# Ranking the first stage's experts on the chip, and putting the second stream's combination behind the first's norm

## The chip, the cores and the metric

The kernel runs on one core of a Trainium2 chip, as one program. Its engines work side by side and wait for one another through semaphores: PE multiplies matrices, DVE and ACT work on rows of data, POOL issues the indirect transfers (gather and scatter of rows by an index table), and SP issues nearly all loads. The metric is device time in microseconds (us), the median of several runs. Each timing of the kernel before lies within about 0.5 us of the median, and 0.2% of it (3.0 us) is taken here as what a measurement can tell from no change.

## The reference

Two layers over 256 latent tokens and 256 context tokens of width 1024, in float32. Each layer is a mixer (conv, pooling, two kinds of attention) and then a mixture of experts, whose router sends each token to 2 of 16 experts. Only the latent stream is returned, so the second layer's mixture works on 256 tokens, and the first's on 512.

```python
for i in range(DEPTH):
    last = i == DEPTH - 1
    ...
    h2 = modulate(rms_norm(x, norm2[i]), sh2[:, None], sc2[:, None])
    tok = h2.reshape(b * n_lat, d)
    if not last:
        tok = jnp.concatenate([tok, h2c.reshape(b * n_ctx, d)], axis=0)
    y2 = moe_ffn(tok, w_router, b_router, w_gate[i], w_up[i], w_down[i])
    x = x + g2[:, None] * y2[:b * n_lat].reshape(b, n_lat, d)
...
# moe_ffn, for one block of tokens of expert e:
a = xblk @ w_gate[e]
u = xblk @ w_up[e]
y = (jax.nn.silu(a) * u) @ w_down[e]
```

An expert's three matrices are 1024x1024 in float32, 4 MB each: 12 MB an expert, 192 MB a layer. Which tokens an expert gets is data; the order in which the experts are worked off is free.

## The kernel before, in words

**The weights.** The class `Ring` (L983) streams the expert weights through 11 units of 2 MB each in the on-chip memory, so it holds a little under two experts. An expert is 12 loads of 1 MB: 4 pairs of gate and up, then 4 of down. All loads go through SP in program order, and `big_load` (its transfers are at L176) lets at most four be in flight: a load is issued when the one four before it has landed, and when the work that read the unit's old content is done. `ring.to(6 * e + 17)` behind expert e lets the stream run on to expert e + 2. SP and PE therefore run as a stream with a buffer between them, and the experts come in the order 0 to 15.

**The work of an expert in the first layer** (`moe0`, L1025). Tokens are handled in tiles of 32. For a tile, POOL gathers the rows of `h2d` (L1043), DVE transposes them (L1051), PE multiplies with gate and up (`gate_up`, L1014), ACT and DVE make silu(a) * u (L1020 to L1022), PE multiplies with down (L1066), ACT copies the result (L1054) and POOL scatters it to `yd` (L1047). Two tiles are always done. A third is done under a branch `v > 64` (L1128), a fourth under `v > 96` (L1133), and rest loops under `v > 128` (L1136). A light expert, with 64 tokens or fewer, takes the other arm of the first branch. Every engine takes these branches by itself, from counts that it has read into registers. [...]

**The router** (`router`, L792). For the last tile of tokens (`choose`, n = 3) DVE picks the experts, PE counts, and DVE turns the counts into the index tables `ig` (rows to gather) and `isx` (rows to scatter to). Then every engine reads 17 counts (L790) and branches on the largest one (L965), before expert 0 begins. DVE's work here and SP's work everywhere stand in the written order; on the other engines, and on DVE elsewhere, a scheduler orders the instructions.

**Behind the first layer's experts.** SP loads the second layer's constants (L260 to L276), parts of its input weights (`w_in`) and of the modulation weights (`w_mod`), then the four tiles of `yd` (L1164) once the last scatter has landed. `combine` (L1169) scales and adds a tile's two expert results, multiplies by a gate (L1173) and adds it to the stream (L1174). `attn_layer(1)` then takes the stream's norm: ACT squares and sums (L364), DVE makes the reciprocal root (`rsqrt`, L152 to L158), ACT scales (L369), PE transposes (L375) and DVE scales the columns (L383). It does so for stream 0 (tiles 0 and 1, latent) and then stream 1 (tiles 2 and 3, context).

**The end.** The second layer's experts (`moe1`, L1180) are another stream of 192 MB through the same ring.

Of the kernel before, what the change touches and what calls it, by code (L numbers as in the profile page):

```python
# [23 lines left out]
NE = 16  # L24
# [17 lines left out]
C_W = 1400  # L42
# [7 lines left out]
def const_layer(layer):  # L50
# [23 lines left out]
    c[:, C_II:C_II + 16] = (64 if layer else 32) * np.arange(16)[None, :]  # L74
    for i in range(4):
        for k in range(2):
            c[:, C_AV + 2 * i + k] = 128 * i + p + 1 if layer else 2 * (128 * i + p) + k + 1
# [22 lines left out]
def dit_moe_kernel(ctx: ExitStack, tc, x, c, cctx_tok, c_ctx, w_mod, b_mod, norm1, norm2, w_in, conv_w, w_pool,  # L100
# [50 lines left out]
    def rsqrt(y, v, hv, t):  # L151
# [3 lines left out]
        for _ in range(3):  # L155
            V.tensor_tensor(t, y, y, op=ALU.mult)
            V.tensor_tensor(t, t, hv, op=ALU.mult)
            V.scalar_tensor_tensor(y, t, 1.5, y, op0=ALU.subtract, op1=ALU.mult)  # L158
# [150 lines left out]
    def attn_layer(L, K, win_a, mid, prefetch, combine):  # L309
# [50 lines left out]
        scaled = None  # L360
        for s in order:
            for i in (2 * s, 2 * s + 1):
                scr = combine(i)
# [3 lines left out]
            rsqrt(stats(8 + k, 2), stats(4 + k, 2), stats(12 + k, 2), stats(16 + k, 2))  # L367
# [424 lines left out]
    def router(L, K, ts, H2):  # L792
# [6 lines left out]
        o = [2424 if L else C_W]  # L799
# [33 lines left out]
        else:  # L833
# [3 lines left out]
            tu = ru(3, 64)  # L837
        def select(e, pair, k):
# [32 lines left out]
        def choose(n, lg, shift):  # L871
# [26 lines left out]
            else:  # L898
                V.tensor_copy(cnt_i[:, 0:16], pp[:, 16:32])
                V.tensor_reduce(cnt_i[:, 16:17], cnt_i[:, 0:16], axis=AX.X, op=ALU.max)  # L900
            pv = pp[:, 0:16]
# [37 lines left out]
        def finish(full):  # L939
# [8 lines left out]
            V.tensor_scalar(ti, pb, -1.0, 0.0, op0=ALU.add, op1=ALU.max)  # L948
            V.tensor_scalar(ti, ti, -2, None, op0=ALU.bitwise_and)
            V.tensor_scalar(ig, ti, 2.0, CS[:, C_PG:C_PG + 1], op0=ALU.mult, op1=ALU.add)  # L950
# [9 lines left out]
            rows(pb, 0, I0, tu[:, 0], tu[:, 1])  # L960
# [3 lines left out]
            counts = read_counts(cnt_i, 512)  # L964
            with tc.If(counts[NE] > 32 * I0):  # L965
# [12 lines left out]
                rows(ps[:, 0:n], I0, I, m1[:, 0:n], m1[:, n:2 * n])  # L978
            return dict(counts=counts, ig=ig, isx=isx, gwt=gwt, pg=pg, at={i: n for n, i in enumerate(ts)})
# [3 lines left out]
    class Ring:  # L983
        def __init__(self, L):
# [3 lines left out]
            self.n = 0  # L988

        def to(self, n):  # L990
# [34 lines left out]
    def moe0(r, ring, tail, tables, late):  # L1025
        counts, ig, isx, gwt, pg, at = (r[n] for n in ("counts", "ig", "isx", "gwt", "pg", "at"))
# [75 lines left out]
        def fetch(e):  # L1102
            for i in range(3):
                gather(h2d, gi(i, e), i)
# [15 lines left out]
        for e in range(NE):  # L1120
            with tc.manual_schedule():
                v = counts[e]
# [46 lines left out]
        def combine(i):  # L1169
# [206 lines left out]
```

## Time and profile before

| | |
|---|---|
| median of the runs | 1521.66 us (1521.1 to 1522.02) |
| profiled execution, own time | 1518.51 us |
| its span, first to last instruction | 1516.9 us |
| PE busy | 1272.8 us, 84% |
| DVE, ACT, POOL busy | 32%, 16%, 11% |
| moved by the transfer engines | 513.45 MB, mean 338 GB/s |
| mean granted TensorE clock | 0.934 of full speed |

Busy shares are means over stages with different limits. What matters is, in each stage, whether the weights' stream runs at its full rate (then its GB/s stands at about 420 and PE waits for loads), or whether PE is behind it and the stream waits for units.

### The profile page before, as it was taken

To read this page: it belongs to the slowest core of one execution; us is meant where nothing else is said; L and a number is where in the kernel's file an instruction comes from. 1 tells how busy PE (TensorE), PEld (TensorE's weight loads), DVE (VectorE), ACT (ScalarE), POOL (GpSimd) and SP (SyncE) were. 2 spreads that over 40 slices of the span, in tenths; PEclk is the share of its full clock that TensorE was granted. 3 is DMA by queue.
4 is the path that set the end of the run, shared out by engine and by line. 5 is a ranking of instruction groups with operands and counts; after the bars stand their busy time and mean duration, and the time that the engine had idled before them with its cause. 6 is when DMAs were issued, how large, how long until landed. Compare 5 with 4: busy or idle time off the path is not lost. (4 is left out here: it accounts for less than half of the span.)

```text
span 1516.9 us, 24606 instructions
## 1 busy us (share of the span) xinstructions
PE 1272.8 (84%) x10006; PEld 595.2 (39%) x10006; DVE 492.7 (32%) x1360; ACT 236.0 (16%) x536; POOL 171.1 (11%) x271
## 2 busy tenths in 40 slices
PE   4998999969888877599999579998889798876778
PEld 1754555533333332244355247744223232221223
DVE  3465366671111111111111377857212221211211
ACT  4342134110000000000000255531000000000000
POOL 0411200002202111121212230300000000000000
PEclk9999979989999999899999779999999998999899
DMA  9677883466999999999988865376999999999995
GB/s 372 219 288 267 280 319 128 164 250 228 419 420 419 419 416 417 418 419 416 417 359 358 286 254 170 136 301 227 368 419 420 372 419 420 419 421 420 417 420 236
DMA packets 92828, 513.45 MB, mean 338 GB/s; under 512 B 16208, under 2 KB 19664, under 8 KB 36816
## 3 DMA queue, kind: packets, MB, share of 16 engines
q1 hardware_dynamic: 84320, 490.47, 80.8%
q0 software_dynamic: 6016, 16.98, 3.0%
q10 hardware_dynamic: 2288, 3.37, 0.6%
q8 instruction: 117, 1.92, 0.5%
q14 instruction: 87, 0.71, 0.1%
HBM read 502.46 MB, written 8.32 MB: 337 GB/s over the span
## 5 line engine op out<-in xcount | busy, mean ns | idle before, releaser
L1014 PE MATMUL psg<-u,W 128*32 128x512 f32 x4032 | 470.8, 611 | 71.8 <-DMA u<-in_w_up_dram 62.4
L1014 PEld LDWEIGHTS psg<-u,W 128*32 128x32 f32 x4032 | 151.0, 112 | 362.2 <-issue 311.3
L1021 DVE TENSOR_TENSOR W<-W,psg 128x256 f32<-128x256 f32 x63 | 26.5, 421 | 561.1 <-ACT W L1020 478.0
L1066 PE MATMUL pd<-u,W 128*32 128x256 f32 x2496 | 160.9, 399 | 41.8 <-issue 23.2
L1066 PEld LDWEIGHTS pd<-u,W 128*32 128x32 f32 x2496 | 93.1, 114 | 110.9 <-issue 54.5
L1216 PE MATMUL pd<-u,x 128*64 128x512 f32 x544 | 128.1, 626 | 2.5 <-DMA u<-in_w_gate_dram 1.9
L1020 ACT ACTIVATE W<-psg 128x256 f32<-128x256 f32 x63 | 24.2, 384 | 516.4 <-PE psg L1014 515.2
L754 PE MATMUL ps<-u,u 128*128 128x512 f32 x192 | 86.8, 598 | 0.0
L848 PE MATMUL pg<-W,x 128*32 128x256 f32 x544 | 46.0, 486 | 45.4 <-DVE x L840 39.1
L1047 POOL DMA_INDIRECT yd<-W x39 | 38.9, 998 | 385.4 <-ACT W L1054 345.6
L211 PE MATMUL psm<-u,W 128*32 128x512 f32 x320 | 48.5, 684 | 34.9 <-DMA u<-in_w_mod_dram 22.0
L1216 PEld LDWEIGHTS pd<-u,x 128*64 128x64 f32 x544 | 40.2, 145 | 86.0 <-issue 84.4
L1043 POOL DMA_INDIRECT W<-h2d,W x54 | 52.1, 965 | 118.7 <-DVE u L932 92.8
L326 DVE TENSOR_TENSOR x<-u,x 128x512 fp32r<-128x512 f32 (+2 forms) x64 | 42.1, 660 | 43.7 <-ACT x L325 39.3
L848 PEld LDWEIGHTS pg<-W,x 128*32 128x32 f32 x544 | 22.6, 130 | 73.0 <-issue 44.0
L325 ACT CAST x<-u 128x512 fp32r<-128x512 f32 (+2 forms) x64 | 35.4, 561 | 99.8 <-PE ps L400 48.6
L1051 DVE STREAM_TRANSPOSE W<-W 128x256 f32<-128x256 f32 x49 | 28.5, 627 | 68.5 <-PE pd L1066 45.9
L754 PEld LDWEIGHTS ps<-u,u 128*128 128x128 f32 x192 | 34.7, 190 | 37.2 <-issue 36.8
L1218 DVE SCALAR_TENSOR_TENSOR W<-pd,W,x 128x512 f32<-128x512 f32 x17 | 12.8, 751 | 111.5 <-PE pd L1216 111.5
L401 PE MATMUL ps<-u,x 128*128 128x512 f32 (+1 forms) x128 | 44.9, 351 | 1.5 <-DVE x L326 1.3
L399 PE MATMUL ps<-u,x 128*128 128x512 f32 (+1 forms) x128 | 45.1, 352 | 0.0
L400 PE MATMUL ps<-u,x 128*128 128x512 f32 (+1 forms) x128 | 44.4, 347 | 0.0
(276 smaller groups left out, 1347.3 us busy)
## 6 DMA issues: line engine op xcount, KB each, us to landing
u<-in_w_gate_dram SPq DMA_DIRECT2D x128, 1024.0 KB
u<-in_w_up_dram SPq DMA_DIRECT2D x128, 1024.0 KB
u<-in_w_down_dram SPq DMA_DIRECT2D x128, 1024.0 KB
u<-in_w_mod_dram SPq DMA_DIRECT2D x40, 1024.0 KB
u<-in_w_in_dram SPq DMA_DIRECT2D x12, 1024.0 KB
x<-in_w_mod_dram SPq DMA_DIRECT2D x8, 1024.0 KB
u<-in_w_out_dram SPq DMA_DIRECT2D x4, 2048.0 KB
u<-m_dram POOLq DMA_DIRECT2D x9, 512.0 KB, 8.8
```

Of the source, the lines that this page charges most:

```text
L211: PE.matmul(ps[32 * g:32 * g + 32, :], sc[:, j, :], t[:, 512 * g:512 * g + 512], start=(j == 0), stop=(j == 7), tile_position=(0, 32 * g))
L326: eng.tensor_tensor(l, src, h.bitcast(F32), op=ALU.subtract)
L399: PE.matmul(ps, xh, yh, start=first, stop=False)
L400: PE.matmul(ps, xh, yl, start=False, stop=False)
L401: PE.matmul(ps, xl, yh, start=False, stop=end)
L754: PE.matmul(ps, CT[:, k, 128 * i:128 * i + 128], wout[hh][:, k, :], start=(k == 0), stop=(k == 7))
L848: PE.matmul(pg[32 * g:32 * g + 32, 256 * i:256 * i + 256], OHG[k][:, c_, 32 * i:32 * i + 32].bitcast(F32), H2[c_][:, 256 * g:256 * g + 256 ...
L1014: PE.matmul(pss[k][32 * g:32 * g + 32, :], xTs[k][:, j, :], w[:, :, 256 * g:256 * g + 256], start=(j == 0), stop=(j == 7), tile_position=( ...
L1043: G.indirect_dma_start(out=XG[b], out_offset=None, in_=src, in_offset=bass.IndirectOffsetOnAxis(ap=ic, axis=0))
L1047: return G.indirect_dma_start(out=dst, out_offset=bass.IndirectOffsetOnAxis(ap=ic, axis=0), in_=src, in_offset=None)
L1066: PE.matmul(pd[32 * g:32 * g + 32, 0:256], hT[:, j, :], w[:, 256 * g:256 * g + 256], start=(j == 0), stop=(j == 7), tile_position=(0, 32 * g))
L1216: PE.matmul(pd[64 * h:64 * h + 64, :], HT[k][:, j, :], w[:, 512 * h:512 * h + 512], start=(j == 0), stop=(j == 7), tile_position=(0, 64 * h))
```

## The change

Experts 0 and 1 stay in front, since their weights are loaded before the router has run. The other 14 are ranked on the chip by their number of tokens, and take the places 2 to 15 in the order: most, fewest, second most, second fewest, and so on. DVE makes a permutation matrix `P`, and with it permutes the counts and the columns of both index tables; the experts' numbers in their new order go to SP, which reads them into registers and addresses the weights by them. Expert 0's first gathers use a small table `ig0` made ahead of the ranking. The 17 counts are no longer read before expert 0: the largest one is read there (`most`), and the 16 counts, now in the new order, behind expert 0's first down product; expert 0's branch has no hint any more. In the second layer's norm, the first DVE operation of `combine` for tiles 2 and 3 is ordered behind the last operation of stream 0's `rsqrt`; that sets an order on DVE and adds no wait.

```diff
+    c[:, C_RK:C_RK + 16] = np.where(q < 2, q, np.where(q % 2 == 0, 1 + q // 2, 16 - q // 2))[None, :]
...
-                scr = combine(i)
+                scr = combine(i, normed) if last else combine(i)
...
-            rsqrt(stats(8 + k, 2), stats(4 + k, 2), stats(12 + k, 2), stats(16 + k, 2))
+            normed = rsqrt(stats(8 + k, 2), stats(4 + k, 2), stats(12 + k, 2), stats(16 + k, 2))
...
+                V.tensor_copy(cf, pp[:, 16:32])
+                V.tensor_reduce(cmax, cf, axis=AX.X, op=ALU.max)
+                V.scalar_tensor_tensor(key, cf, 16.0, e16, op0=ALU.mult, op1=ALU.add)
+                for e in range(2):
+                    V.tensor_scalar(key[:, e:e + 1], key[:, e:e + 1], (2 - e) * 65536.0, None, op0=ALU.add)
...
+            rows_in(ig0, pb[:, 0::16], ti[:, 0:4])
+            V.tensor_copy(cnt_i[:, 16:17], cmax)
...
+            V.tensor_tensor(cmp, pair(key, 1), pair(key, 0), op=ALU.is_gt)
+            V.tensor_reduce(rank, cmp, axis=AX.X, op=ALU.add)
+            V.tensor_tensor(P, pair(CS[:, C_RK:C_RK + 16], 0), pair(rank, 1), op=ALU.is_equal)
+            for src, dst, a, b in ((e16, eid, -1.0, 16.0), (cf, cnt_i[:, 0:16], 1.0, 0.0)):
+                V.tensor_tensor(cmp, P, pair(src, 1), op=ALU.mult)
+                V.tensor_reduce(tot, cmp, axis=AX.X, op=ALU.add)
+                V.tensor_scalar(dst, tot, a, b, op0=ALU.mult, op1=ALU.add)
+            order = nc.values_load_multi_w_load_instructions(
+                eid[0:1, 0:16], engines=(ET.SP,), min_val=0, max_val=15,
+                skip_runtime_bounds_check_because="a permutation of the experts")[1]
+            pbs = tu[:, 1]
+            for i in range(I0):
+                V.tensor_tensor(cmp, P, pair(pb[:, 16 * i:16 * i + 16], 1), op=ALU.mult)
+                V.tensor_reduce(pbs[:, 16 * i:16 * i + 16], cmp, axis=AX.X, op=ALU.add)
+            rows_in(ig, pbs, ti)
...
-            counts = read_counts(cnt_i, 512)
-            with tc.If(counts[NE] > 32 * I0):
+            most = nc.values_load_multi_w_load_instructions(cnt_i[0:1, NE:NE + 1], min_val=0, max_val=512)[1][0]
+            with tc.If(most > 32 * I0):
...
-                src = dict(g=w_gate, u=w_up, d=w_down)[nm][self.L, e].rearrange("(p j) n -> p j n", j=8)[:, 2 * h:2 * h + 2, :]
+                at = ds(self.order[e], 1) if self.order and e > 1 else slice(e, e + 1)
+                src = dict(g=w_gate, u=w_up, d=w_down)[nm][self.L, at].rearrange("o (p j) n -> p (o j) n", j=8)[:, 2 * h:2 * h + 2, :]
...
-                gather(h2d, gi(i, e), i)
+                gather(h2d, gi(i, e) if e else ig0[:, i:i + 1], i)
...
-                tc.mark_branch_hint_location(f"more{e}", v > 64, engines=[ET.PE])
+                if e:
+                    tc.mark_branch_hint_location(f"more{e}", counts[e] > 64, engines=[ET.PE])
                 gu(e, [0, 1], [0, 1], [None, None])
                 dn(e, 0, "t")
-                with tc.If(v > 64, label=f"more{e}") as cmp:
+                if not e:
+                    counts.extend(r["read"]())
+                v = counts[e]
+                with tc.If(v > 64, **({"label": f"more{e}"} if e else {})) as cmp:
...
-            V.scalar_tensor_tensor(t, Yt[i][:, 1], gwt[:, 1, at[i]:at[i] + 1], t, op0=ALU.mult, op1=ALU.add)
+            j = V.scalar_tensor_tensor(t, Yt[i][:, 1], gwt[:, 1, at[i]:at[i] + 1], t, op0=ALU.mult, op1=ALU.add)
+            if before is not None:
+                behind(j, before)
```

Three places where the order of instructions moves. First, DVE between the router and expert 0. Before, it reads the counts and branches, and only then makes the three transposes of expert 0's first tiles (the rows between are the branch's body, for a count over 128):

```order
L963 COPY st<-u_63 128x1
L790 TENSOR_LOAD st
L965 COMPARE_AND_BRANCH
...
L965 UNCONDITIONAL_BRANCH x2
L1051 STREAM_TRANSPOSE W<-W 128x256 x3
```

In the change, two of the transposes (now L1101) stand in the middle of the ranking (L978 to L984 rank and permute, L990 and L991 permute the index table), well ahead of the read (L1006) and the branch:

```order
L978 TENSOR_TENSOR W<-u_63 128x256
L979 TENSOR_REDUCE W<-W 128x16
L980 TENSOR_TENSOR W<-u_63,W 128x256
L982 TENSOR_TENSOR W<-W,u_63 128x256
L983 TENSOR_REDUCE W<-W 128x16
L984 TENSOR_SCALAR W<-W 128x16
L982 TENSOR_TENSOR W<-W,u_63 128x256
L1101 STREAM_TRANSPOSE W<-W 128x256
L983 TENSOR_REDUCE W<-W 128x16
L984 TENSOR_SCALAR st<-W 128x16
L990 TENSOR_TENSOR W<-W,pb 128x256
L1101 STREAM_TRANSPOSE W<-W 128x256
```

So the transposes no longer wait for the counts, but the second one has more of DVE's work ahead of it.

Second, PE at expert 0. Before, the read and the branch come ahead of its first product with gate and up (L1014):

```order
L927 MATMUL pb<-W,u_63 128x64 x2
L790 TENSOR_LOAD st
L1125 REGISTER_ALU
L1371 BRANCH_PREFETCH_HINT
L965 COMPARE_AND_BRANCH
```

In the change (gate and up L1062) the first products stand ahead of the read of the largest count, and the others behind its branch:

```order
L944 MATMUL pb<-W,u_63 128x64 x2
L1062 MATMUL psg<-u_71,W 32x512 x8
L1062 MATMUL psg<-u_6_1290,W 32x512 x4
L1062 MATMUL psg<-u_71,W 32x512 x4
L1062 MATMUL psg<-u_6_1290,W 32x512
L1006 TENSOR_LOAD st
L1007 COMPARE_AND_BRANCH
```

The read moved from ahead of PE's products into their midst. Behind the first down product (L1116) there is a second read, of the 16 counts, ahead of a branch (L1181) without a hint:

```order
L1116 MATMUL pd<-u_69,W 32x256 x16
L1116 MATMUL pd<-u_67,W 32x256 x16
L1024 TENSOR_LOAD st
L1181 COMPARE_AND_BRANCH
```

Third, DVE in the second layer's first norm. Before, the 12 small steps of stream 0's `rsqrt` (L152 to L158) lie among the long operations of `combine` for tiles 2 and 3 (L1172 to L1174 on u_64):

```order
L152 TENSOR_SCALAR st<-st 128x2
L154 TENSOR_SCALAR st<-st 128x2
L1174 TENSOR_TENSOR x_7_1291<-x_7_1291,u_64 128x1024
L153 TENSOR_SCALAR st<-st 128x2
L1172 SCALAR_TENSOR_TENSOR u_64<-u_73,st,u_64 128x1024
L156 TENSOR_TENSOR st<-st 128x2
L1173 TENSOR_TENSOR u_64<-u_64,u_67 128x1024
L157 TENSOR_TENSOR st<-st 128x2
L1174 TENSOR_TENSOR x_8_1292<-x_8_1292,u_64 128x1024
L158 SCALAR_TENSOR_TENSOR st<-st 128x2
```

In the change the steps (now L155 to L161) stand together, and five long operations (L1225 to L1229) follow ahead of stream 0's column scaling (L393, before L383):

```order
L161 SCALAR_TENSOR_TENSOR st<-st 128x2
L1225 SCALAR_TENSOR_TENSOR u_64<-u_64,st 128x1024
L1225 SCALAR_TENSOR_TENSOR u_64<-u_73,st,u_64 128x1024
L1228 TENSOR_TENSOR u_64<-u_64,u_67 128x1024 x2
L1229 TENSOR_TENSOR x_7_1291<-x_7_1291,u_64 128x1024
L393 TENSOR_SCALAR u_73<-pt,ab 128x256 x8
L1229 TENSOR_TENSOR x_8_1292<-x_8_1292,u_64 128x1024
```

So the norm's end moves ahead of them, and the column scaling stays behind all but one.

## Rows read from the trace of the kernel before

**Rows 1.** Busy time by stretch; columns: stretch, length, each engine, PEclk, DMA share, GB/s.

```profile
364.80:751.60 386.80, 317.75 (x3631) 134.33 (x3627) 51.63 (x94) 21.19 (x56) 69.55 (x98) 0.95 1.01 417
788.20:858.90 70.70, 60.41 (x776) 34.73 (x776) 13.08 (x31) 6.92 (x18) 15.63 (x38) 0.96 0.85 323
887.00:1050.00 163.00, 152.19 (x802) 103.25 (x803) 118.96 (x359) 71.56 (x167) 26.55 (x35) 0.98 0.56 206
1075.00:1500.00 425.00, 347.57 (x2589) 114.79 (x2584) 79.11 (x191) 17.90 (x38) 0.00 (x0) 0.93 1.00 413
```

**Rows 2.** Timeline of SP, weight loads; columns: start us, length us, instruction.

```profile
364.83 0.57 SPq L176 DMA_DIRECT2D u<-in_w_gate_dram  x1
...
558.68 0.33 SPq L176 DMA_DIRECT2D u<-in_w_gate_dram  x1
...
580.55 8.04 SPq L176 DMA_DIRECT2D u<-in_w_down_dram  x4
590.79 0.33 SPq L176 DMA_DIRECT2D u<-in_w_gate_dram  x1
...
751.63 0.33 SPq L176 DMA_DIRECT2D u<-in_w_gate_dram  x1
...
788.18 0.37 SPq L176 DMA_DIRECT2D u<-in_w_gate_dram  x1
...
809.95 16.01 SPq L176 DMA_DIRECT2D u<-in_w_down_dram  x4
```

**Rows 3.** Timeline of POOL in the first layer's experts, gathers and scatters.

```profile
440.51 0.97 POOL L1043 DMA_INDIRECT W<-h2d,W  x1 [0.30 <-issue]
...
605.07 1.00 POOL L1047 DMA_INDIRECT yd<-W  x1 [3.96 <-ACT W L1054]
...
647.12 1.00 POOL L1047 DMA_INDIRECT yd<-W  x1 [13.82 <-ACT W L1054]
...
815.33 0.97 POOL L1043 DMA_INDIRECT W<-h2d,W  x1 [0.30 <-issue]
...
852.46 0.97 POOL L1047 DMA_INDIRECT yd<-W  x1 [4.76 <-ACT W L1054]
```

**Rows 4.** Costliest groups of instructions, the page's own: the scatters.

```profile
L1047 POOL DMA_INDIRECT yd<-W x39 | 38.9, 998 | 385.4 <-ACT W L1054 345.6
```

**Rows 5.** Timeline of DVE between the router and expert 0.

```profile
336.22 0.42 DVE L917 TENSOR_TENSOR u<-u 128x256 f32<-128x256 f32 x1
...
342.95 0.63 DVE L1051 STREAM_TRANSPOSE W<-W 128x256 f32<-128x256 f32 x1 [1.83 <-DVEq L965]
```

**Rows 6.** Timeline of PE: behind a branch in expert 4, and behind moe1's read of counts.

```profile
479.03 3.21 PE L1066 MATMUL pd<-u,W 128*32 128x256 f32 x26 [4.32 <-issue]
...
1065.98 3.31 PE L848 MATMUL pg<-W,x 128*32 128x256 f32 x32 [3.20 <-DVE x L840]
```

**Rows 7.** Timeline of SP behind the first layer's last weights.

```profile
827.89 0.33 SPq L260 DMA_DIRECT2D u<-in_cst_dram  x1
...
848.28 1.88 SPq L176 DMA_DIRECT2D u<-in_w_mod_dram  x2
858.90 3.17 SPq L1164 DMA_DIRECT2D u<-yd  x4
```

**Rows 8.** Timeline of ACT in the second layer's first norm.

```profile
874.94 0.19 ACT L364 ACTIVATION_READ_ACCUMULATOR u<-x 128x1 f32 x1
...
882.78 2.19 ACT L369 ACTIVATE W<-x,st 128x1024 f32<-128x1024 f32 x2 [6.62 <-DVE st L158]
```

**Rows 9.** Timeline of DVE in the same place.

```profile
877.71 1.28 DVE L1172 SCALAR_TENSOR_TENSOR u<-u,st,u 128x1024 f32<-128x1024 f32 x1
...
882.39 0.16 DVE L157 TENSOR_TENSOR st<-st 128x2 f32<-128x2 f32 x1
882.59 0.16 DVE L158 SCALAR_TENSOR_TENSOR st<-st 128x2 f32<-128x2 f32 x1
885.96 1.90 DVE L383 TENSOR_SCALAR u<-pt,ab 128x256 f32<-128x256 f32 x4 [3.22 <-PE pt L375]
```

More of the change, by code (lines that the diff above doesn't have):

```diff
@@ L41 @@
 C_DT = 1144
-C_W = 1400
+C_RK = 1400
+C_W = 1416
 def const_table():
@@ L157, in rsqrt, with behind @@
             V.tensor_tensor(t, t, hv, op=ALU.mult)
-            V.scalar_tensor_tensor(y, t, 1.5, y, op0=ALU.subtract, op1=ALU.mult)
+            i = V.scalar_tensor_tensor(y, t, 1.5, y, op0=ALU.subtract, op1=ALU.mult)
+        return i
+    def behind(i, before):
+        tc.add_manual_dep(i.ins, before.ins.name,
+                          mybir.DependencyInfo(mybir.DependencyClass.NoSync, mybir.DependencyReason.SCHED_ONLY),
+                          reason="the first stream goes ahead")
     def rsqrt1(y, v, hv, t):
@@ L958, in rows @@
                 V.tensor_tensor(isx[:, 16 * i0:16 * i1], tv, tz, op=ALU.add)
-            rows(pb, 0, I0, tu[:, 0], tu[:, 1])
+            rows(pbs, 0, I0, tu[:, 0], tu[:, 2])
             gate_weights(NT - 1)
@@ L977, in finish @@
                 m1 = M1a.rearrange("p t k n -> p (t k n)")
-                rows(ps[:, 0:n], I0, I, m1[:, 0:n], m1[:, n:2 * n])
-            return dict(counts=counts, ig=ig, isx=isx, gwt=gwt, pg=pg, at={i: n for n, i in enumerate(ts)})
+                for i in range(I - I0):
+                    V.tensor_tensor(cmp, P, pair(ps[:, 16 * i:16 * i + 16], 1), op=ALU.mult)
+                    V.tensor_reduce(m1[:, 2 * n + 16 * i:2 * n + 16 * i + 16], cmp, axis=AX.X, op=ALU.add)
+                rows(m1[:, 2 * n:3 * n], I0, I, m1[:, 0:n], m1[:, n:2 * n])
+            read = lambda: nc.values_load_multi_w_load_instructions(cnt_i[0:1, 0:NE], min_val=0, max_val=512)[1]
+            return dict(read=read, order=order, ig0=ig0, ig=ig, isx=isx, gwt=gwt, pg=pg, at={i: n for n, i in enumerate(ts)})
         return choose, finish
@@ L988, in __init__ @@
             self.n = 0
+            self.order = None
         def to(self, n):
@@ L1025, in moe0 @@
     def moe0(r, ring, tail, tables, late):
-        counts, ig, isx, gwt, pg, at = (r[n] for n in ("counts", "ig", "isx", "gwt", "pg", "at"))
+        order, ig0, ig, isx, gwt, pg, at = (r[n] for n in ("order", "ig0", "ig", "isx", "gwt", "pg", "at"))
+        counts = []
+        ring.order = order
         XG = [W[:, 256 * k:256 * k + 256] for k in range(4)]
@@ L1167, in moe0, with combine @@
                   cond_at(2304, 2048), loads)
-        def combine(i):
+        def combine(i, before=None):
             t = tmp[i]
             S.activation(t, Yt[i][:, 0], AF.Copy, scale=gwt[:, 0, at[i]:at[i] + 1])
-            V.scalar_tensor_tensor(t, Yt[i][:, 1], gwt[:, 1, at[i]:at[i] + 1], t, op0=ALU.mult, op1=ALU.add)
+            j = V.scalar_tensor_tensor(t, Yt[i][:, 1], gwt[:, 1, at[i]:at[i] + 1], t, op0=ALU.mult, op1=ALU.add)
+            if before is not None:
+                behind(j, before)
             V.tensor_tensor(t, t, g2b[i // 2], op=ALU.mult)
```

21 lines of the change are left out of this document (15 added, 6 removed).

## The prediction

> **What bounds the kernel now.** I read busy time by stretch first. From 364.8 to 751.6 us the transfer engines move 417 GB/s and PE works 317.75 of 386.80 us [rows 1]: the weights' stream binds, and PE has 69 us to spare. From 788.2 to 858.9 us PE works 60.41 of 70.70 us and the stream falls to 323 GB/s: there PE is behind, and the stream waits for it. From 887 to 1050 us (second layer's attention) PE works 152.19 of 163.00 us at 206 GB/s, so whatever starts that stretch earlier ends it earlier. From 1075 us the stream binds again, at 413 GB/s. It starts from a full ring whose units PE has freed, so I take it to move with the end of the attention.
>
> Why PE is behind at 788 us is read on POOL: a third gather behind the first scatter marks an expert with a third tile. There are six such rows, the first at 440.51 us in expert 3, the others in experts 10 to 14, the last at 815.33 us [rows 3]. The 39 scatters [rows 4] are 16 x 2 + 6 + 1, so one of the six has a fourth tile. Five dense experts follow one another at the end. Measured from an expert's own first gate load to its second scatter, expert 8, with two tiles and PE ahead, takes 605.07 - 558.68 = 46.4 us; expert 15, with two tiles as well, takes 852.46 - 788.18 = 64.3 us [rows 2, 3]. The 17.9 us between are PE's arrears, and they are the prize.
>
> What ends last behind the experts: SP issues the four `yd` loads at 858.90 us, 6.4 us after the last scatter [rows 3, 7], and all of the second layer's norm hangs on them.
>
> **The change, part by part.** The sum goes along the weights' stream: when it starts, how long it runs, what PE adds behind it.
>
> *Start of the stream.* Expert 2's first gate load goes out at 364.83 us [rows 2]: the ring is full until PE has passed expert 0's branch. All that delays PE in expert 0 delays everything, with no cover. Three things do. (a) DVE's ranking: some eight 128x256 operations and reductions of about 0.42 us [rows 5] lie around the two transposes. Before, DVE waited 1.83 us there for the counts and made the first transpose at 342.95 us [rows 5]. That wait is gone, and about 3 us of new work comes ahead of the first transpose, of which the gather's landing hides most. The second transpose slips by about one operation, 0.4 us. DVE's other new work, some 7 us, lies under PE's first gate and up products, before DVE is needed again; without that cover it would cost its full length. (b) PE's read of the largest count, now amid its products: between nothing (if its queue holds enough work) and 1.83 us, the wait of DVE for 17 values; I take 1.0. (c) PE's read of 16 counts and a branch without a hint, behind the first down product. The nearest row is `moe1`, which reads 17 counts at the same place: PE stood for 3.20 us [rows 6]. Part of that was DVE's work, so 0 to 3.2; I take 2.6. [...] Together 4.0 us; bounds 0.4 and 0.4 + 1.8 + 3.2 + 4.3 = 9.7.
>
> *Length of the stream.* From expert 2 to expert 14 the first gate loads go from 364.83 to 751.63 us, 12 steps of 32.23 us [rows 2], or 2.69 us a load. Gathers and scatters are the same number as before, so I keep this step. Place 15 then starts at 364.83 + 4.0 + 13 x 32.23 = 787.8 us, where expert 15 started at 788.18: the stream itself hardly gains. For this PE has to free units in time. Before, two dense experts in a row (13 with four tiles, 14) held expert 15's four down loads for 16.01 us instead of expert 8's 8.04 [rows 2]; five in a row were needed for PE to get that far behind. With each dense expert between light ones, and PE's 69 us to spare, I take no hold; for the four-tile expert at place 2, with little prefetched behind it, up to 3 us.
>
> The 168 loads of places 2 to 15 now take their address from a register. No row shows such a load. SP needs 0.33 us for a load and has 2.69, with three others in flight, so a slower issue is covered. I take nothing; the other end is a rival below.
>
> *Behind the stream.* Place 15 is light, with light ones at 13 and 14, so PE is ahead of the stream there. Its second scatter comes 46.4 us after its first gate load [rows 2, 3]: 787.8 + 46.4 = 834.2 us, and the `yd` loads 6.4 us later, at 840.6 instead of 858.90 us: **-18.3 us**. Bounds: if the other arm's code comes late, expert 9 is the row, 647.12 - 590.79 = 56.3 us [rows 2, 3].
>
> That uncovers SP's own work. Expert 8's last down load is out 580.55 + 8.04 - 558.68 = 29.9 us after its first gate load [rows 2], so place 15's at 817.7 us. Constants, input weights and modulation loads follow; from 827.89 to 850.16 us they took 22.3 us [rows 7], which gives 840.0 us, just under 840.6. Before, SP was done 8.7 us early. And the 5 MB of big loads at the end of this block (12.5 us at 417 GB/s [rows 1]) go out from about 833 us, so they are in transfer until about 845.5 us, ahead of the first `yd` tile. Between 0 and 4.9 us; I take the middle, **+2.5 us**.
>
> *The norm's order.* ACT's last square of stream 0 ends at 875.13 us, but its scaling starts at 882.78 us, waiting for DVE's L158 [rows 8]: the `rsqrt` steps lie among operations of 1.28 us. Alone, a step takes 0.20 us [rows 9]: 13 steps give 877.7 us, 5.0 us earlier. Then five long operations of 1.25 us go ahead of the column scaling, to 884.0 us, where PE's transposes would allow 877.7 + 3.2 = 880.9. The scaling began at 885.96 us [rows 9], so **-2.0 us**; bounds 0 (stream 1 becomes late) and -5.0.
>
> Sum: -18.3 + 2.5 - 2.0 = -17.8 us. The profiled execution goes from 1518.51 to 1500.7 us. The median of the runs was 3.1 us above the profiled execution; from it the forecast is 1521.66 - 17.8 = **1503.9 us**. With all bounds good it is -3.6 - 2.5 - 3.0 = -9.1 more, 1495; with all bad +5.7 + 3.0 + 9.9 + 2.4 + 2.0 = +23.0, 1527.
>
> **The rivals.**
>
> *A: PE is late at the end all the same, by its code.* In expert 4 PE stops for 4.32 us with no wait that the profile shows [rows 6], and expert 9 needs 56.3 - 46.4 = 9.9 us more than expert 8 [rows 2, 3] on the same arm. Both are light experts, which jump over the third tile's code. The change puts light experts at places 13, 14 and 15; a stop at 14 is mostly covered, since place 15 waits for its loads, a stop at 15 is not. Against it: expert 8 takes the same arm with nothing lost. With 9.9 us lost there and bound (c) at its worst, +5.7, the time is 1503.9 + 9.9 + 5.7 = 1519.5; with one of the two 1510 to 1514. [...]
>
> *B: loads with an address from a register run slower, and the kernel with them.* This one ends on the other side. For it: no row shows such a load, and 168 of them lie on the binding stream. Against it: shape and size of the transfers stay, and the issue has cover. It decides from 17.8 / 168 = 0.106 us a load, 4% of 2.69. At 0.2 us a load the stream takes 33.6 us more, and the time is 1537.
>
> *C: the gain ends at the norm.* The second layer's loads, which went out in PE's arrears, now lie ahead of `yd` and its input weights. At worst the 12.5 us of big loads and SP's 8.7 us of lost lead come fully onto the path, 21.2 us against the -18.3 and -2.0: no change, 1522.6. Against it: `yd` is asked for behind these loads, not with them, and most of them have landed by then.
>
> **How the numbers follow.** The forecast (a gain of 10 to 27 us) gets 0.66, A 0.16, C 0.08, B 0.10. The likeliest case has its own range, 1495 to 1512. The range for 8 in 10 takes in A, and reaches from 1493 to 1519.5; above lie B and most of C. Faster by over 0.2% (3.0 us, about what a measurement of this kernel can tell from no change): 0.66 + most of A = 0.81; within 0.2%: 0.09; slower: 0.10.
>
> **What would show it.** After: expert 2's first gate load at about 369 us; then steps of 32.2 us and 417 GB/s to the last weight; the last scatter at about 834 us and 46 us after its place's first gate load; the `yd` loads at about 841 us; ACT's scaling 2.6 us behind its last square; and the stretches behind it as long as before. The prediction is wrong if the step is above 33 us (B), if PE is idle for over 6 us in expert 0 or stops in place 15 (A), or if `yd` lands more than 10 us after it is asked for (C).

## The result

The changed kernel takes 1505.63 us (median of 4 runs, 1501.66 to 1508.32) against 1521.82 us before (4 runs, 1521.10 to 1522.02): ratio 0.9895, 95% interval 0.9877 to 0.9913, 16.2 us less. In the experiments' 17 to 23 runs each the kernel before went from 1515.1 to 1525.2 us; single runs scatter more than those first four show, so a difference of 3 us between two medians of a few runs says little. A difference given below behind a ratio is worked out from that ratio; it is not the ratio of the two medians, which can stand some us further apart.

The profiled execution of the changed kernel took 1505.54 us, its span 1504.0. Its rows that answer to [rows 1, 2, 3, 7, 8, 9] follow; those of PE's stops, for [rows 6], stand with e6_reads and under rival A. First the busy time by stretch, with [rows 1]'s columns (stretch, length, PE, PEld, DVE, ACT, POOL, PEclk, DMA share, GB/s): the stream from place 2 to place 14, place 15, and the second layer's attention.

```profile
363.90:753.40 389.50, 348.77 (x4056) 156.29 (x4052) 55.18 (x101) 23.78 (x63) 76.34 (x107) 0.96 1.01 415
786.80:838.00 51.20, 34.22 (x408) 13.98 (x400) 6.94 (x20) 2.83 (x8) 8.62 (x30) 0.87 0.86 334
872.90:1035.00 162.10, 150.56 (x803) 101.55 (x803) 121.57 (x363) 72.19 (x167) 26.86 (x35) 0.99 0.58 213
```

The stream's rate is the one of before. In place 15 PE is no longer behind: it works 34 of 51 us, where it worked 60 of 71. SP's timeline (start us, length us, instruction), to set against [rows 2, 7]:

```profile
363.88 0.35 SPq L185 DMA_DIRECT2D u<-in_w_gate_dram  x1
...
417.26 11.00 SPq L185 DMA_DIRECT2D u<-in_w_down_dram  x4
...
753.41 0.33 SPq L185 DMA_DIRECT2D u<-in_w_gate_dram  x1
...
786.82 0.33 SPq L185 DMA_DIRECT2D u<-in_w_gate_dram  x1
...
806.93 8.29 SPq L185 DMA_DIRECT2D u<-in_w_down_dram  x4
815.27 0.43 SPq L269 DMA_DIRECT2D u<-in_cst_dram  x1
...
833.45 0.98 SPq L185 DMA_DIRECT2D u<-in_w_in_dram  x2
834.98 1.06 SPq L1207 DMA_DIRECT2D u<-m_dram  x2
...
837.54 2.75 SPq L185 DMA_DIRECT2D u<-in_w_mod_dram  x2
844.03 2.56 SPq L1217 DMA_DIRECT2D u<-yd  x4
```

Place 15's four down loads go out in 8.29 us, where PE had held expert 15's for 16.01. The `yd` loads go out 14.9 us earlier. The last scatter, on POOL [rows 3], is earlier by more, 20.96 us:

```profile
831.50 0.97 POOL L1097 DMA_INDIRECT yd<-W  x1 [3.52 <-ACT W L1104]
```

So 12.5 us lie between the last scatter and the `yd` loads, where 6.4 lay before. The waits of SP from 780 to 875 us (in total, times, longest) say for what; first the kernel before, then the changed one:

```profile
SPq L1164 <- DMA yd<-W: 4.3, 1, 4.3
```

```profile
SPq L1217 <- DMA u<-m_dram: 4.6, 2, 3.7
```

Before, the scatter ended last; now it is a load of `m_dram` (a broadcast row, `g2b`), issued ahead: in the trace the first `yd` load waits 3.7 us for the semaphore that this load raises. ACT and DVE in the norm, for [rows 8, 9]:

```profile
853.85 1.15 ACT L1224 ACTIVATE u<-u,st 128x1024 f32<-128x1024 f32 x1 [7.93 <-DMA u<-yd]
...
863.60 0.19 ACT L374 ACTIVATION_READ_ACCUMULATOR u<-x 128x1 f32 x1
...
866.18 2.19 ACT L379 ACTIVATE W<-x,st 128x1024 f32<-128x1024 f32 x2 [1.35 <-DVE st L161]
```

```profile
871.85 3.46 DVE L393 TENSOR_SCALAR u<-pt,ab 128x256 f32<-128x256 f32 x7
```

The first `yd` tile is used 9.8 us after SP asks for it. ACT's scaling comes 2.4 us behind its last square (7.65 before), the column scaling 14.1 us earlier than before. PE's first projection, the first product of the second layer's attention, in the changed kernel and in the one before:

```profile
872.88 0.50 PE L409 MATMUL ps<-u,u 128*128 128x512 f32 x1 [0.66 <-DVE u L393]
```

```profile
887.00 0.79 PE L399 MATMUL ps<-u,u 128*128 128x512 f32 x1 [0.43 <-DVE u L383]
```

Two rows of PE's timeline, of the changed kernel and of the one before, show a difference that no step of the prediction has: the router's last product (`pb`) comes 6.2 us earlier, before the ranking has begun.

```profile
330.68 1.12 PE L944 MATMUL pb<-W,u 128*128 128x64 f32 x4 [2.29 <-DVE W L939]
```

```profile
336.89 1.11 PE L927 MATMUL pb<-W,u 128*128 128x64 f32 x4 [1.96 <-DVE W L922]
```

The difference of the two spans, 12.9 us, along the chain (each term is a difference of two intervals between such rows):

| interval | before | after | difference | forecast |
|---|---|---|---|---|
| start to `pb` | 336.89 | 330.68 | -6.2 | 0 |
| `pb` to PE's first gate product | 6.75 | 6.32 | -0.4 | 0 |
| to expert 2's first gate load | 21.19 | 26.88 | +5.7 | +4.0 |
| to the last scatter | 487.63 | 467.62 | -20.0 | -22.3 |
| to the `yd` loads | 6.44 | 12.53 | +6.1 | 0 |
| to the first combination (ACT L1224) | 6.30 | 9.82 | +3.5 | +2.5 |
| to PE's first projection | 21.80 | 19.03 | -2.8 | -2.0 |
| to the second experts' first product | 168.71 | 167.42 | -1.3 | 0 |
| to the end | 461.19 | 463.70 | +2.5 | 0 |

### The profile page after: what moved, and what is told of

It is laid out like the page before. It is cut to its first block, busy times and chain, and to the rows that moved or that the text cites. A ratio compares the mean times of both kernels' runs of the same rounds, so it can differ in the third digit from the quotient of the medians.

```text
span 1504.0 us, 24971 instructions
## 1 busy us (share of the span) xinstructions
PE 1275.2 (85%) x10006; PEld 592.1 (39%) x10006; DVE 498.7 (33%) x1384; ACT 236.9 (16%) x536; POOL 172.0 (11%) x271
## 3 DMA queue, kind: packets, MB, share of 16 engines
q8 instruction: 118, 1.93, 0.5%
## 5 line engine op out<-in xcount | busy, mean ns | idle before, releaser
L1062 PE MATMUL psg<-u,W 128*32 128x512 f32 x4032 | 465.6, 607 | 47.6 <-DMA u<-in_w_up_dram 37.3
L1062 PEld LDWEIGHTS psg<-u,W 128*32 128x32 f32 x4032 | 145.2, 111 | 338.2 <-issue 296.0
L1116 PE MATMUL pd<-u,W 128*32 128x256 f32 x2496 | 167.8, 413 | 49.4 <-issue 32.8
L1116 PEld LDWEIGHTS pd<-u,W 128*32 128x32 f32 x2496 | 96.6, 118 | 122.2 <-issue 74.1
L1101 DVE STREAM_TRANSPOSE W<-W 128x256 f32<-128x256 f32 x49 | 28.4, 625 | 80.7 <-PE pd L1116 52.2
L411 PE MATMUL ps<-u,x 128*128 128x512 f32 (+1 forms) x128 | 44.6, 348 | 1.5 <-DVE x L335 1.3
L409 PE MATMUL ps<-u,x 128*128 128x512 f32 (+1 forms) x128 | 45.3, 354 | 0.0
L1104 ACT COPY W<-pd 128x256 f32<-128x256 f32 x39 | 14.5, 372 | 195.5 <-PE pd L1116 195.5
```

What stands on the lines that cost most here:

```text
L409: PE.matmul(ps, xh, yh, start=first, stop=False)
L411: PE.matmul(ps, xl, yh, start=False, stop=end)
L1062: PE.matmul(pss[k][32 * g:32 * g + 32, :], xTs[k][:, j, :], w[:, :, 256 * g:256 * g + 256], start=(j == 0), stop=(j == 7), tile_position=( ...
L1116: PE.matmul(pd[32 * g:32 * g + 32, 0:256], hT[:, j, :], w[:, 256 * g:256 * g + 256], start=(j == 0), stop=(j == 7), tile_position=(0, 32 * g))
```

## The experiments

Each kernel was timed beside the kernel before, and profiled once. This table has the same intervals for all; its numbers are differences of rows like those above.

| kernel | `pb` at | product to load | load to last scatter | scatter to `yd` | `yd` to combination |
|---|---|---|---|---|---|
| e1_after | 329.59 | 27.15 | 465.65 | 12.12 | 9.80 |
| e2_table | 332.38 | 20.45 | 488.33 | 6.17 | 6.03 |
| e3_norm | 338.23 | 21.39 | 489.67 | 6.02 | 4.72 |
| e4_static | 335.10 | 20.54 | 467.09 | 11.86 | 10.39 |
| e5_ident | 331.80 | 29.28 | 487.02 | 5.88 | 4.93 |
| e6_reads | 329.51 | 21.97 | 466.35 | 12.03 | 9.90 |
| e7_g2b | 329.57 | 27.75 | 465.75 | 6.04 | 12.18 |
| e8_win | 330.41 | 27.10 | 465.84 | 5.93 | 9.89 |
| e9_descend | 331.96 | 28.64 | 476.27 | 11.75 | 9.51 |
| e10_reads_win | 331.57 | 22.27 | 466.58 | 5.91 | 9.63 |
| e11_reads_g2b | 330.96 | 22.45 | 465.03 | 6.21 | 12.22 |

**e1_after: the changed kernel again.**

> The changed kernel itself, beside the kernel before on the same chip and beside the three parts. 1505.6 us again (ratio 0.9895). In its trace the router's product of positions (pb) ends near 330.7 us, against 336.9 us before, although no line of the change speaks of the first layer's attention. Theory O (the first layer's attention runs in another order, and that is worth about 6 us): 330.7 us again. Theory N (noise of one execution): anything from 330 to 337 us.

1506.39 us against 1520.27; ratio 0.9918 (0.9902 to 0.9933), a gain of 10.2 to 14.9 us. `pb` is at 329.59 us again, so this is not the noise of one execution.

**e2_table: only the wider table.** The edit, in the kernel before:

```diff
-C_W = 1400
+C_W = 1416
```

> The kernel before with only the table of constants widened from 1400 to 1416 columns; nothing reads the new columns. Theory O: the wider table alone gives the first layer's matmuls the order that the changed kernel has (122 of TensorE's 894 places ahead of pb hold another row), and with it 6 us: about 1515.6 us, pb at about 330.7 us. The prediction's theory, which gave the attention nothing: 1521.8 us, pb at 336.9 us.

1514.15 us, ratio 0.9969 (0.9955 to 0.9983): 4.7 us less (2.6 to 6.8), with `pb` at 332.38 us. Sixteen columns that nothing reads make the kernel faster (the router's scratch behind the table moves by as many columns). The compiler's scheduler gives the first layer's matmuls another order: of the 1373 in the trace up to `pb`, 129 places hold another one than before, and all 1373 are the same in e2_table and in the changed kernel. One place where it shows is in the waits of PE from 100 to 122 us, where PE's transposes wait for DVE (the kernel before, then e2_table):

```profile
PE pt L573 <- DVE u L566: 3.5, 1, 3.5
```

```profile
PE pt L573 <- DVE u L566: 1.5, 1, 1.5
```

Over all kernels, `pb` stands at 335.1 to 338.2 us in the three with the old order (before, e3, e4; mean 336.7), and at 329.5 to 332.4 us in the ten profiles with the new one (mean 330.8). Theory O holds, but not all of these 5.9 us are the order's. From the first place that differs (the 312th matmul) to the first behind the last (the 821st) it takes 102.7 to 104.2 us in the three and 98.9 to 100.6 in the ten, 4.3 us less in the mean; the rest lies outside these places, where the order is the same. The wait above is 2.0 of the 4.3 us. PE's own work is 1.9 more, as busy time by stretch shows for these places (the kernel before, then e2_table): the same matmuls, at a mean granted clock (PEclk) of 0.98 and of 1.00.

```profile
84.50:188.40 103.90, 97.97 (x511) 53.36 (x510) 54.09 (x129) 31.63 (x74) 19.34 (x18) 0.98 0.80 279
```

```profile
85.47:184.72 99.25, 96.06 (x511) 52.83 (x510) 51.00 (x129) 31.55 (x74) 19.38 (x18) 1.00 0.84 294
```

**e3_norm: only the norm's order** (`behind` and its calls, added to the kernel before).

```diff
-                scr = combine(i)
+                scr = combine(i, normed) if last else combine(i)
```

> The kernel before with only the order of the second layer's norm (the second stream's combination behind the first's rsqrt). The prediction's term: -2.0 us, bounds 0 and -5.0: 1519.8 us, ACT's scaling 2.6 us or less behind its last square. The rival reading of the changed trace (the edit brings ACT 5.2 us and PE 2.8 us): 1519.0 us. If stream 1 becomes late behind it: 1521.8 us.

1518.72 us, ratio 0.9990 (0.9976 to 1.0003): 1.5 us less, between 3.6 less and 0.5 more; alone it can't be told from nothing by the clock. The rows can tell it: ACT's scaling comes 1.35 us behind DVE's L158 where it waited 6.62 [rows 8], and PE's first projection (885.92 us) comes 9.1 us behind the last square, against 11.9 before: 2.8 us.

```profile
876.63 0.19 ACT L371 ACTIVATION_READ_ACCUMULATOR u<-x 128x1 f32 x1
876.72 1.13 ACT L1178 ACTIVATE u<-u,st 128x1024 f32<-128x1024 f32 x1
879.21 2.19 ACT L376 ACTIVATE W<-x,st 128x1024 f32<-128x1024 f32 x2 [1.35 <-DVE st L158]
```

**e4_static: the alternation without its machinery.** The order is a list in the program, made for these inputs; the ranking is left out.

```diff
+PLACE = (0, 1, 13, 5, 14, 7, 11, 9, 12, 8, 3, 6, 10, 2, 4, 15)
...
-                src = dict(g=w_gate, u=w_up, d=w_down)[nm][self.L, e].rearrange(
+                src = dict(g=w_gate, u=w_up, d=w_down)[nm][self.L, e if self.L else PLACE[e]].rearrange(
...
-                v = counts[e]
+                v = counts[PLACE[e]]
```

> The kernel before with the norm's order, and with the order of the experts that the ranking finds for these inputs written into the kernel as a list: no ranking, no loads with an address from a register, counts read at once and expert 0's hint as before. By the prediction's terms (-18.3 without the 4.0 us of the start is -22.3, +2.5 for the backlog, -2.0 for the norm): 1500.0 us. Theory O: the alternation and the norm alone brought 16.2 - 6 us less what the ranking costs at the start (4 to 7.6 us), so -14 to -18: 1504 to 1508 us, unless SP's own work, which ends last, takes what the earlier end of the experts gives: then 1508 to 1510 us.

1505.02 us, ratio 0.9909 (0.9892 to 0.9925): 13.8 us less, as theory O says; the prediction's terms had said 1500.0 us. Its loads have fixed addresses, and from expert 2's load to the last scatter it takes 467.09 us; the changed kernel, with 168 addresses from a register, took 467.62 and 465.65. These addresses cost nothing. Its `pb` is at 335.10 us, in the old order, so the alternation and the norm's order make their gain without the new one. And here too SP asks for `yd` 11.9 us behind the scatter, so that this delay doesn't come with the ranking. Nor does it come with an early end as such: in e9_descend the last scatter is late (843.44 us) and the delay is 11.75 us. It comes where the last scatter follows soon on SP's last weight load: 16 us behind that load's issue here and in e9_descend, 26.5 us in the kernel before. The rows of e4_static:

```profile
829.46 0.97 POOL L1055 DMA_INDIRECT yd<-W  x1 [3.02 <-ACT W L1062]
```

```profile
835.00 2.63 SPq L183 DMA_DIRECT2D u<-in_w_mod_dram  x2
841.32 2.54 SPq L1172 DMA_DIRECT2D u<-yd  x4
```

**e5_ident: the machinery without the alternation.**

```diff
-                V.scalar_tensor_tensor(key, cf, 16.0, e16, op0=ALU.mult, op1=ALU.add)
+                V.scalar_tensor_tensor(key, cf, 0.0, e16, op0=ALU.mult, op1=ALU.add)
...
-    c[:, C_RK:C_RK + 16] = np.where(q < 2, q, np.where(q % 2 == 0, 1 + q // 2, 16 - q // 2))[None, :]
+    c[:, C_RK:C_RK + 16] = q[None, :]
```

> The changed kernel with everything that the ranking needs (its operations, the reads, the loads with an address from a register, the wider table, the norm's order), but with a key that leaves the counts out and a table of places that counts upwards, so that the experts run in their old order. Prediction: the start costs 4.0 us and the addresses nothing, so expert 2's first gate load comes 25.2 us behind PE's first gate product (21.2 before), and the last scatter 487.6 us behind that load as before; the time is that of the table alone (1514.2) + 4.0 - 2.0, about 1516. From the changed trace: the start costs 5.7, so 26.9 us, and the time is about 1518. Rival B (an address from a register costs 0.1 us a load or more): over 17 us more between load and scatter, 1530 or more.

1517.17 us, ratio 0.9982 (0.9965 to 0.9999): 2.7 us less. From product to load it takes 29.28 us instead of 21.19, more than both theories said. From load to scatter it takes 487.02 us, the old length with register addresses: rival B falls a second time.

```profile
367.49 0.35 SPq L185 DMA_DIRECT2D u<-in_w_gate_dram  x1
```

```profile
854.51 0.97 POOL L1097 DMA_INDIRECT yd<-W  x1 [5.70 <-ACT W L1104]
```

**e6_reads: all counts read ahead of expert 0, and expert 0's hint kept.** The hint is the instruction of PE that `mark_branch_hint_location` puts ahead of a branch.

```diff
-            most = nc.values_load_multi_w_load_instructions(cnt_i[0:1, NE:NE + 1], min_val=0, max_val=512)[1][0]
+            known = read_counts(cnt_i, 512)
+            most = known[NE]
...
-                if e:
-                    tc.mark_branch_hint_location(f"more{e}", counts[e] > 64, engines=[ET.PE])
+                tc.mark_branch_hint_location(f"more{e}", counts[e] > 64, engines=[ET.PE])
```

> The changed kernel with its counts read all at once ahead of expert 0, and with expert 0's hint, as in the kernel before. If the prediction's terms (b) and (c) hold, 3.6 us of the start go away: expert 2's first gate load 23.3 us behind PE's first product, 1502.8 us. If the read must then wait for DVE's ranking with PE idle ahead of expert 0, PE's first product comes 3 to 7 us later instead, and the time is 1506 to 1510 us.

1503.25 us, ratio 0.9897 (0.9872 to 0.9922). The timeline of PE in expert 0, for the kernel before, the changed kernel and then e6_reads:

```profile
343.64 16.38 PE L1014 MATMUL psg<-u,W 128*32 128x512 f32 x128 [5.63 <-DVE W L1051]
359.84 7.24 PE L1066 MATMUL pd<-u,W 128*32 128x256 f32 x128
```

```profile
337.00 16.62 PE L1062 MATMUL psg<-u,W 128*32 128x512 f32 x128 [5.20 <-DVE W L1101]
354.78 3.66 PE L1116 MATMUL pd<-u,W 128*32 128x256 f32 x64 [1.16 <-issue]
361.67 6.44 PE L1116 MATMUL pd<-u,W 128*32 128x256 f32 x64 [3.22 <-issue]
```

```profile
329.51 1.12 PE L944 MATMUL pb<-W,u 128*128 128x64 f32 x4 [2.29 <-DVE W L939]
339.06 16.56 PE L1063 MATMUL psg<-u,W 128*32 128x512 f32 x128 [8.43 <-DVE u L991]
355.89 7.11 PE L1117 MATMUL pd<-u,W 128*32 128x256 f32 x128 [0.27 <-PE psg L1063]
```

The two stops, 1.16 and 3.22 us, and the broken run of down products are gone: from product to load it takes 21.97 us. The break costs more than its stops. Behind the second one, the changed kernel's 64 down products take 6.44 us where the 64 ahead of it took 3.66, and the granted clock (busy time by stretch) is 0.56 of full speed in the mean, where it was 1.00:

```profile
354.78:358.50 3.72, 3.66 (x64) 2.36 (x64) 0.86 (x2) 0.00 (x0) 0.23 (x2) 1.00 0.11 35
361.67:368.11 6.44, 6.44 (x68) 3.59 (x72) 1.70 (x3) 0.00 (x0) 0.00 (x0) 0.56 0.69 255
```

e6_reads moves the read and puts the hint back at once, so which of the two the stops belong to is not shown. Both expectations were half right, since PE now waits for DVE's permuting ahead of the first product (8.43 us, 3.3 more from `pb` to product than in e1_after). The net is 1.9 us (product to load 5.2 less, less 3.3).

**e7_g2b: `g2b` between the `yd` loads.**

```diff
-        for k in range(2):
-            SP.dma_start(g2b[k], bcast_row(m_dram[0, k, 5120:6144], 1024))
...
+                    if i % 2:
+                        SP.dma_start(g2b[i // 2], bcast_row(m_dram[0, i // 2, 5120:6144], 1024))
                     SP.dma_start(Yt[i], yd[1024 * i:1024 * i + 1024].rearrange("(p k g) f -> p k (g f)", k=2, g=4))
```

> The changed kernel with the two broadcast loads of m_dram (g2b, 1 MB) moved from ahead of the modulation weights to between the yd loads. Theory L (SP's first yd load waits for the landing of the g2b load eight places ahead of it, in whose semaphore lane it goes, not for the scatter): SP asks for yd about 7 to 8 us behind the last scatter instead of 12, as soon as its own issues are out, and the first combination starts 4 to 6 us earlier: about 1501 us. Rival Q (the transfers queued ahead set when yd lands, whenever it is asked for): only the 1 MB counts, 2.5 us: 1504 us. Rival G (g2b, now behind the first yd tile, becomes the last that the combination waits for): 1506 us or more.

1504.75 us, ratio 0.9893 (0.9869 to 0.9918). SP asks for the first `yd` tile 6.04 us behind the scatter, so theory L is right about the wait; but ACT has the tile 12.18 us later, and starts 3.0 us earlier than in e1_after, not the 4 to 6 of theory L but about the 2.5 us of rival Q:

```profile
835.41 0.33 SPq L1217 DMA_DIRECT2D u<-yd  x1
```

```profile
847.59 1.15 ACT L1224 ACTIVATE u<-u,st 128x1024 f32<-128x1024 f32 x1 [6.42 <-DMA u<-yd]
```

The wait for `g2b` is real, but next to nothing is won by asking earlier: the first `yd` tile is then used 12.18 us after SP asks for it, where e1_after took 9.80.

**e8_win: the input weights behind `yd`.**

```diff
-            todo = {1: (0, 1, 2, 3), 3: (4,)}.get(j, ())
+            todo = {1: (0, 1, 2, 3, 5), 3: (4,)}.get(j, ())
...
+                elif i == 5:
+                    first()
```

(`first` is the load of the input weights' first two parts, which was in `tail0`.)

> The changed kernel with the first two loads of the second layer's input weights (2 MB) moved behind the yd loads. Theory Q (backlog): 2 MB at 417 GB/s are 5.0 us, so the first combination starts about 5 us earlier and the time is about 1501.5 us; the g2b loads land as much earlier, so SP's wait for them goes too. Rival W: the splits of the input weights, now late, hold the first projection, and the time stays at 1506 us or goes above it.

1504.15 us, ratio 0.9900 (0.9877 to 0.9923). With 2 MB less ahead the first combination starts 5.2 us earlier than in e1_after, where theory Q said 5.0:

```profile
835.50 3.59 SPq L1219 DMA_DIRECT2D u<-yd  x4
```

```profile
845.39 1.15 ACT L1226 ACTIVATE u<-u,st 128x1024 f32<-128x1024 f32 x1 [7.02 <-DMA u<-yd]
```

PE's first projection comes 5.6 us earlier (863.97 us), so rival W's hold ahead of it is refuted; but the second experts' first product comes only 2.2 us earlier (1036.86). The stretch between them needs care, since its length goes with the granted clock: over all profiles but e8 and e10 it takes 167.3 us at a mean clock of 0.98 and 173.1 at 0.94. At e8's 0.97 the kernel before takes 168.71 us, 4.2 less than e8 (the kernel before, then e8_win):

```profile
887.00:1055.71 168.71, 156.70 (x842) 105.35 (x842) 123.99 (x387) 71.56 (x167) 26.55 (x35) 0.97 0.54 200
```

```profile
863.97:1036.86 172.89, 159.25 (x858) 104.70 (x858) 129.26 (x391) 71.54 (x167) 27.41 (x35) 0.97 0.58 213
```

PE has 16 more products in it, 2.5 us more of work, and stops 1.9 us for a later load (`in_mla_w_uq_dram`), a wait that only e8 and e10 (1.4 us) have. So the loads put behind `yd` do take most of the gain back, only later than rival W says.

**e9_descend: dense experts first, in a run.** Only the table of places is another: `c[:, C_RK:C_RK + 16] = q[None, :]`.

> The changed kernel with another table of places: the ranking as before, but the experts with many tokens one after another from place 2 on (110, 93, 91, 87, 67, 65 tokens), then the light ones. Theory S (a run of dense experts puts PE behind, a full ring then holds the stream, and a held stream never catches up; it does not matter where the run lies): SP's loads are held for PE by some 12 to 18 us in places 4 to 9, the last scatter comes 45 us behind place 15's first gate load, but 12 to 18 us later than with the alternation, and the time is 1516 to 1522 us, all of the alternation's gain lost. Rival E (only the last experts matter, since PE's 69 us to spare make up for the rest): last scatter at 829 to 832 us and 1506 us, the same as the alternation.

1519.01 us, ratio 0.9984 (0.9967 to 1.0002): nearly all of the gain in time is gone. Last scatter at 843.44 us, 10.6 us further behind expert 2's load than in e1_after. Busy time by stretch, and one of SP's waits from 360 to 860 us, in e9_descend and then in the changed kernel:

```profile
440.00:480.00 40.00, 39.25 (x464) 18.06 (x460) 4.96 (x9) 2.27 (x6) 10.09 (x14) 1.00 0.93 379
480.00:520.00 40.00, 35.70 (x418) 15.79 (x412) 5.99 (x11) 2.65 (x7) 7.11 (x10) 0.96 0.96 392
...
720.00:760.00 40.00, 30.93 (x300) 11.46 (x304) 3.89 (x7) 1.51 (x4) 6.44 (x10) 0.87 1.01 420
```

```profile
SPq L185 <- PEq L1186: 30.9, 5, 8.2
```

```profile
SPq L185 <- PEq L1186: 5.9, 2, 5.7
```

In the run PE is busy for 39.25 of 40 us and the stream falls to 379 GB/s; at 720 us PE has 9 us to spare in 40, and the stream is back at 420, about its rate wherever PE is not behind, and no faster. Theory S: the held stream did not catch up, with the run at the front as with the run at the end; other places were not tried. Its size was a little overrated (10.6 us, where 12 to 18 was said), and of the 20 us that the alternation brings between load and scatter about half stays. That half is used up by the start (28.64 us from product to load, 21.19 before) and by the delay of the `yd` loads, which is there all the same.

**e10_reads_win and e11_reads_g2b: versions that join two gains.** e10 is e6_reads with the input weights behind the second `yd` tile, e11 is e6_reads with e7_g2b's edit.

> The changed kernel with the counts read at once ahead of expert 0 (as in e6_reads) and the first two loads of input weights behind the second yd tile (e8_win put them behind the fourth). If the two gains add: 1.8 us at expert 2's first gate load, yd asked for 6 us instead of 12 us behind the last scatter, first combination at 843 to 844 us, second layer's first gate product at 1033 to 1034 us, and a time of 1500 to 1501 us. If the late weights take back what the earlier norm gives, as most of it in e8_win: 1502 to 1503 us.

> The changed kernel with the counts read at once and the g2b loads between the yd loads (e6_reads and e7_g2b together). If the two gains add: yd asked for 6 us behind the last scatter, first combination at 845 to 846 us, 1501 to 1502 us. If g2b behind the first yd tile costs what the earlier yd brings: 1503 us.

e10: 1503.07 us, ratio 0.9888 (0.9867 to 0.9908); e11: 1501.58 us, ratio 0.9886 (0.9868 to 0.9903). Both have the short start (22.3 and 22.5 us) and the early request for `yd` (5.9 and 6.2 us). Their intervals overlap with those of the changed kernel, so that e11 has the lowest median here, 4.8 us under e1_after's, but is not shown to be better. e11 came out as its first expectation says (1501 to 1502 us), e10 near its second. In e10 the loads put behind `yd` take back most of it again: first combination 4.9 us earlier than in e1_after, second experts' first product 1.2 us (1037.91), and from first projection to there 173.6 us at a granted clock of 0.96, where e1_after takes 169.5 at the same clock.

## Why the prediction was right, step by step

The time came within 2 us of the forecast. In part that is luck: the traces show two errors of opposite sign, 4 to 6 us that the first layer's attention gained and the sum left out, and 7 us more than forecast on the way from the last scatter to the first combination. The gain of 17.8 us itself was rather too large: the two profiled executions stand 12.9 us apart, and e1_after, timed against more runs, puts it at 10.2 to 14.9 us.

- **Where the kernel starts from.** The sum took the first layer's attention as unchanged. That failed: it ends 4 to 6 us earlier (6.2 in this pair of profiles), and the wider table alone brings 4.7 us (e2_table). Expert 2's first gate load therefore came at 363.88 us instead of about 369, and the place 15 at 786.82 instead of 787.8, although the start cost more than forecast.
- **Start of the stream, +4.0.** Mechanism right, size low: +5.7 and +6.0 in the two profiles of the changed kernel, 5.7 to 8.1 in all six with this reading. Terms (b) 1.0 and (c) 2.6 were the stops of 1.16 and 3.22 us; with the reads in one place ahead of expert 0 and the hint kept, 5 us go away (e6_reads, e10, e11). Of term (a), 0.4, at most 0.2 us shows: PE's gate and up products take 16.62 us instead of 16.38. What the sum lacked is the slower clock behind the stops (64 down products in 6.44 us at 0.56, against 3.66 us at 1.00). The 4.3 us in the upper bound of 9.7 are the length of PE's gap in expert 4 [rows 6]; no run shows them at expert 0, or what PE waited for in that gap: its two stops at expert 0 were 1.16 and 3.22 us here, 2.36 and 2.62 us in e5_ident.
- **Length of the stream, nothing.** Right: 12 steps in 753.41 - 363.88 = 389.5 us are 32.46 us a step, for 32.23, at 415 GB/s. The 2.7 us in all are of the size of the hold that was allowed for the four-tile expert at place 2, and the hold shows: place 3's four down loads take 11.00 us, 3.0 more than expert 8's [rows 2] (417.26 us in SP's timeline). Register addresses cost nothing (467.62 and 465.65 us from load to scatter with them, 467.09 without in e4; in the old order 487.02 with them in e5, 487.63 without).
- **Behind the stream, 46.4 us.** 831.50 - 786.82 = 44.7 us, and PE's arrears are gone. From load to last scatter the alternation brought 20.0 us where 22.3 was said.
- **The `yd` loads 6.4 us behind the scatter.** This step failed. SP was through with its own issues at 840.29 us, where 840.0 had been estimated (its last weight load was out 2.5 us earlier than forecast, and the loads behind it took 25.0 us instead of 22.3), but the scatter came at 831.50 instead of 834.2, and the `yd` load waited 3.7 us more for `g2b`: 12.5 us behind the scatter, not 6.4.
- **Backlog +2.5 us.** Too small, and wrongly kept apart from the step before: the prediction took the middle between no wait and a full one for the bytes in flight when `yd` is asked for. e7 and e8 show the path: SP's last weights, then the small constants one by one, then 5 MB and the first `yd` tile in the order of issue (with 1 MB less ahead of it the first combination starts 3.0 us earlier than in e1_after, with 2 MB less 5.2 us). From the last scatter to the first combination it was 22.3 us instead of 12.7; 9.6 us of the alternation's 20 stayed there.
- **The norm's order, -2.0.** Right in mechanism and nearly in size: -2.8, and e3_norm has 2.8 alone.
- **The stretches behind.** As long as before, within what the granted clock moves: from first projection to the second experts' first product it took 167.42 us at 0.98, and 168.71 at 0.97 before.

**Rival A** didn't decide. PE stopped in place 14 for 4.54 us with no wait that the profile shows, and that was covered; in place 15 for 0.68 us, where the kernel before shows 1.93. The two rows, of PE in the changed kernel:

```profile
800.73 3.59 PE L1116 MATMUL pd<-u,W 128*32 128x256 f32 x26 [4.54 <-issue]
...
829.66 1.07 PE L1116 MATMUL pd<-u,W 128*32 128x256 f32 x15 [0.68 <-issue]
```

The second row took the same arm as the first with hardly a stop, so the arm alone doesn't tell the two apart. That PE waited for its code in the first was the author's guess; no run shows it, there or in experts 4 and 9. **Rival B** is refuted by e4_static and e5_ident. **Rival C** named the right mechanism and came to almost half of its worst, 9.6 of 21.2 us; `yd` landed 9.8 us after it was asked for, just under the mark of 10.

What stays open: why the same instructions take 27 us from product to load in one kernel and 29 in another; why the granted clock of the second layer's attention is 0.94 in one execution and 0.98 in another; and the gain of e11 over the changed kernel. Of the first, the trace of e5_ident shows where the 2 us lie: PE's first stop in expert 0 is 2.36 us instead of 1.16, and the 64 down products behind it take 5.35 us at a mean granted clock of 0.68 instead of 3.66 at 1.00. Why that stop is longer it doesn't show.

## What to carry to other kernels

Where a stream binds and each item's other work varies, look for runs of heavy items: the stream's time was lost here when the ring was full, and no later slack brought it back, with the run at the end or at the front (10.6 us in e9_descend). When a stage ends earlier, follow the queue of the next stage's loads in order of issue: what was hidden under the stage became the path here (9.6 us), and asking earlier for the last item gained little with the bytes ahead of it still there (0.5 us in e7_g2b, beside the 1 MB that it took out of the way). And compare the two traces from the first microsecond on, since an edit can move the scheduler's order far ahead of itself; and the granted clock beside each length, before a few us are put down to an edit.

## What the runs showed of the hardware that was not expected

Sixteen more columns in a table of constants were worth 4.7 us (2.6 to 6.8), through the order that the scheduler gave to 129 of 1373 matmuls. Two stops of PE, of 1.16 and 3.22 us with 3.66 us of products between them, were followed by products at a granted clock of 0.56 instead of 1.00, so that 64 of them took 6.44 us instead of 3.66. The second layer's attention, with the same matmuls, took 167.3 us at a granted clock of 0.98 and 173.1 at 0.94. Loads whose address comes from a register ran as fast as others: 465.7 and 467.6 us against 467.1 for the same stretch.
